# Attention scores of a hybrid decoder trunk: the keys' low halves on all 128 rows, and the low-by-low product added

## The chip, the core and the metric

The kernel runs on one core of a Trainium2 chip. The metric is device time in microseconds (us) of one execution; the time of a kernel is the median of its runs. One execution is also recorded by the hardware profiler; its rows are what this text reads.

## The reference

A decoder trunk of two layers over 512 tokens of width 1024, all in float32. Layer 0 mixes with a gated MLP and an RWKV-7 time mix and ends with a dense SwiGLU. Layer 1 mixes with a sparse attention (eight query heads, two key/value heads of 64 channels, that is, four query heads to a key/value head) and a gated short convolution, and ends with a mixture of eight experts of which each token uses two. What the change touches are the scores of two of the attention's three branches, the selected blocks and the window; with 512 tokens both reach every earlier token, so they differ only in their keys and values:

```python
ss = jnp.einsum('bhgqd,bhqnld->bhgqnl', qr, kg).astype(f32)
ps = _masked_softmax(ss.reshape(...) * scale, ms)
...
sw = jnp.einsum('bhgqd,bhkd->bhgqk', qr, kwb).astype(f32) * scale
pw = _masked_softmax(sw, mw)
```

qr are the queries and kg, kwb the keys, both after a partial rotation by position; a score is a sum over 64 channels.

## The kernel before, in words

TensorE multiplies in a reduced float32 format ("fp32r" in the rows). To keep float32 accuracy, an operand is split: the high half is the value copied into fp32r (on ScalarE), the low half is the difference (a subtraction on VectorE, `split`, line 107). A product is then three matmuls into one PSUM bank, high by high, high by low, low by high (`mm3`, line 125; lines 127 to 129 in the rows).

Layer 1's mix (`layer1_mix`, line 682) runs in this order in the program: constants, projections of keys and queries (`nsa_proj`), two projections that feed the compressed branch (`compress`), then `attend` for four query blocks of 128 tokens (tb = 0 to 3), four blocks of the short convolution (`conv`, three projections each) and the output rows. The program order is not the order in the queues: instructions are traced by a tile framework whose planner orders each engine's queue at build time, by a priority and by when an instruction is ready in its plan, and sets the semaphores. Conv projections therefore stand between score matmuls in TensorE's queue, as fillers (rows with `pmm`, lines 127 to 129).

For a score the 64 channels of a key/value head g lie on one half of the 128 rows. `nsa_proj` and `stacked` (lines 748 and 737) lay out the operands:

- Queries, tile `qq` per head b and key/value head g: the high half of the query lies on the rows of g, its low half on the other 64 rows (copied there by a DMA on the POOL queue, lines 769 and 770).
- Keys' high halves, tile `kk` per branch and g: on the rows of g, and a copy on the other 64 rows (DMAs on POOL, lines 759 and 760).
- Keys' low halves, tile `klo` per branch: one tile of 128 rows in which each g has its own 64 rows.

`attend` (line 805) works through two branches, four heads b and two key/value heads g. A score block is 128 queries by n keys, n = 128, 256, 384, 512 for tb = 0 to 3, and takes two matmuls into one of two PSUM banks `sc`: line 821 on all 128 rows (query high and low, each with the key's high half) and line 822 on the 64 rows of g (query high with key low). There are 64 such pairs, 16 in each query block. VectorE then adds the mask and takes the row minimum (line 824), ScalarE the exponential (826), VectorE scales (834), TensorE transposes (839), ScalarE copies out of PSUM (842), and TensorE multiplies by the values (847).

Weights come through SP's DMA queue into three `wraw` buffers (line 955), in 512 KB units; a unit is split into `whi` and `wlo` (lines 108 and 109) and feeds 24 matmuls. Line 975 in `moe_consts` loads a gain row `grow`, 1024 values spread over 128 rows; `moe_consts` runs before `layer1_mix`, and the row is read only in `router` (lines 1023 and 1026), at the end of layer 1's mix. A tile that shares a tag with another takes its place in memory, so its first write waits for the last reader of the other.

Of the kernel before, what the change touches and what calls it, by code (L numbers as in the profile page):

```python
# [9 lines left out]
F32 = mybir.dt.float32  # L10
F32R = mybir.dt.float32r
# [7 lines left out]
T = 512  # L19
D = 1024  # L20
# [47 lines left out]
class Body:  # L68
# [613 lines left out]
    def layer1_mix(self):  # L682
        nc, tc, I = self.nc, self.tc, self.I
        with ExitStack() as ctx:
            pool = lambda name, bufs, **kw: ctx.enter_context(tc.tile_pool(name=name, bufs=bufs, **kw))
            self.cp1, self.wk1, self.pa = pool("n_const", 1), pool("n_work", 2), pool("n_psum", 1, space=PSUM)
            self.nsa_consts()
            self.nsa_proj()
            self.compress()
            self.acc = [self.cp1.tile([128, 2, T], F32, tag="zc%d" % i, name="acc") for i in range(2)]  # L690
            for tb in range(NTB):
                self.attend(tb)
            yd = [self.conv(b) for b in range(3)]
            self.out_rows(I["w_out1a"][0:2], yd[0:2])
            yd.append(self.conv(3))
            yc = []
            for q in range(4):
                hi = self.cp1.tile([128, T], F32R, tag="q%d" % q, name="ych")
                lo = self.cp1.tile([128, T], F32R, tag="qq%da" % q, name="ycl")
                self.split(hi, lo, self.acc[q // 2][:, q % 2, :])  # L700
                yc.append((hi, lo))
            self.out_last(I["w_out1"], yc, I["w_out1a"][2:4], yd[2:4])
# [34 lines left out]
    def stacked(self, src, lo, name):  # L737
        nc, cp = self.nc, self.cp1
        out = []
        for g in range(2):  # L740
            p = slice(g * 64, g * 64 + 64)
            t = cp.tile([128, T], F32R, name=name + "ab"[g])
            nc.scalar.activation(t[p], src[p], AF.Copy)
            nc.vector.tensor_sub(lo[p], src[p], t[p].bitcast(F32))
            out.append(t)
        return out

    def nsa_proj(self):
        nc, I, cp, wk = self.nc, self.I, self.cp1, self.wk1
        V, S, G = nc.vector, nc.scalar, nc.gpsimd  # L750
        unit = lambda i: self.unit(I["w_in1"][i])
        near, far = slice(0, 64), slice(64, 128)
        self.kk, self.klo = [], []
        pss = self.proj_first([self.ahead[0], self.unit(I["w_in1"][1], G, raw=self.ahead[1])], lambda: self.bank("sc", 2))
        for i in range(2):
            src = self.roped(pss[i], wk.tile([128, T], F32, tag="wA", name="qtmp"))
            lo = cp.tile([128, T], F32R, name="klo%d" % i)
            kk = self.stacked(src, lo, "kk%d" % i)
            nc.gpsimd.dma_start(kk[0][far], kk[0][near])
            nc.gpsimd.dma_start(kk[1][near], kk[1][far])  # L760
            self.kk.append(kk)
            self.klo.append(lo)
        self.qs, self.qq = [], []
        for b in range(4):
            q = cp.tile([128, T], F32, name="q%d" % b)
            src = self.roped(self.proj_block(unit(2 + b)), q)
            lo = wk.tile([128, T], F32R, tag="pt", name="qlo", bufs=PTB)
            qq = self.stacked(src, lo, "qq%d" % b)
            nc.gpsimd.dma_start(qq[0][far], lo[near])
            nc.gpsimd.dma_start(qq[1][near], lo[far])  # L770
            self.qs.append(q)
            self.qq.append(qq)
        self.vsw = cp.tile([128, NTB, 256], F32, name="vsw")
        self.gat = cp.tile([128, NTB, 8, 3], F32, name="gat")
        units = [unit(6 + i) for i in range(3)]
        for tb in range(NTB):
            t = slice(tb * 128, (tb + 1) * 128)
            ps = self.psum()
            for kb in range(KB):
                wh, wl = units[kb // 3]  # L780
                n = slice((kb % 3) * 280, (kb % 3) * 280 + 280)
                self.mm3(ps[:, 0:280], self.xh[:, kb, t], self.xl[:, kb, t], wh[:, n], wl[:, n],
                         kb == 0, kb == KB - 1)
            V.tensor_copy(self.vsw[:, tb, :], ps[:, 0:256])
            S.activation(self.gat[:, tb].rearrange("p h b -> p (h b)"), ps[:, 256:280], AF.Sigmoid)
        self.zc = []
        for j in range(2):
            ps = self.proj_block(unit(9 + j))
            raw = wk.tile([128, T], F32, tag="wA", name="craw")
            S.activation(raw, ps, AF.Copy)  # L790
            z = cp.tile([128, 16, 2, 32], F32, name="zc%d" % j)
            G.memset(z[:, :, :, 31:32], 0.0)
            for g in range(2):
                zp = wk.tile([128, T], F32, tag="wB", name="zp")
                src = raw[g * 64:g * 64 + 64, :]
                nc.sync.dma_start(zp[0:64, :], src)
                nc.sync.dma_start(zp[64:128, 0:T - 1], src[:, 1:T])
                zv = zp.rearrange("p (n l two) -> p l n two", l=8, two=2)[:, :, :, 0]
                for lh in range(2):
                    V.tensor_tensor(z[:, lh * 8:lh * 8 + 8, g, 0:31], zv[:, :, lh:lh + 31],  # L800
                                    self.cpos[:, j, lh * 8:lh * 8 + 8].unsqueeze(2).broadcast_to([128, 8, 31]),
                                    op=ALU.add)
            self.zc.append(z)

    def attend(self, tb):
# [6 lines left out]
        for br in range(2):  # L812
            sm = self.sm.tile([128, 8], F32, name="smm", bufs=2)
            mn = self.sm.tile([128, 8], F32, name="mn", bufs=2)
            pt = [[wk.tile([128, 2, 4, 128], F32, name="pt", bufs=PTB) for _ in range((tb + 2) // 2)] for _ in range(2)]
            for b in range(4):
                es = []
                for g in range(2):
                    i = b * 2 + g
                    ps = self.bank("sc", 2)  # L820
                    mm(ps[:, 0:n], self.qq[b][g][:, t], self.kk[br][g][:, 0:n], start=True, stop=False)
                    mm(ps[:, 0:n], self.qq[b][g][half[g], t], self.klo[br][half[g], 0:n], start=False, stop=True)  # L822
                    e = wk.tile([128, T], F32, name="prob", bufs=4)
                    V.tensor_tensor_reduce(e[:, 0:n], ps[:, 0:n], self.dmask[:, 512 - n:512], scale=-0.125,  # L824
                                           scalar=3e38, op0=ALU.add, op1=ALU.min, accum_out=mn[:, i:i + 1])
                    S.activation(e[:, 0:n], e[:, 0:n], AF.Exp, bias=mn[:, i:i + 1], scale=-1.0,
                                 accum_out=sm[:, i:i + 1])
                    es.append(e)
                rc = sm[:, b * 2:b * 2 + 2]
                V.tensor_scalar(rc, rc, 1e-30, None, op0=ALU.max)  # L830
                V.reciprocal(rc, rc)
                for g in range(2):
                    e = es[g]
                    V.tensor_scalar(e[:, 0:n], e[:, 0:n], rc[:, g:g + 1], self.gat[:, tb, g * 4 + b, br + 1:br + 2],
                                    op0=ALU.mult, op1=ALU.mult)
                    ps = self.bank("tr", 2)
                    for kb in range(tb + 1):
                        k = slice(kb * 128, (kb + 1) * 128)
                        nc.tensor.transpose(ps[:, k], e[:, k], self.ident)
                    for j, d in enumerate(pt[g]):  # L840
                        m = min(2, tb + 1 - 2 * j)
                        S.activation(d[:, 0:m, b, :], ps[:, j * 256:j * 256 + m * 128].rearrange("p (k t) -> p k t", k=m),
                                     AF.Copy)
            for kb in range(tb + 1):
                for g in range(2):
                    c = br * 128 + g * 64
                    mm(po[half[g], :], self.vsw[:, kb, c:c + 64],
                       pt[g][kb // 2][:, kb % 2].rearrange("p b t -> p (b t)"), start=(br == 0 and kb == 0), stop=False)
# [109 lines left out]
    def moe_consts(self, cp):  # L958
# [12 lines left out]
        def load(name, shape, src):  # L971
            t = cp.tile(shape, F32, name=name)
            nc.sync.dma_start(t, src)
            return t
        self.grow = load("grow", [128, D], I["o_norm_ffn"].broadcast_to([128, D]))
        wr = load("wr", [128, KB, 8], I["w_router"])
        gcol = load("gcol", [128, KB], I["ffn_gain"])
        self.wr = cp.tile([128, KB, 32], F32, name="wrg")
# [623 lines left out]
```

## Time and profile before

| | |
|---|---|
| median of 3 runs | 1592.73 us (1589.03 to 1598.78) |
| the profiled execution | 1590.39 us |
| its span, first to last instruction | 1588.6 us, mean granted TensorE clock 0.983 |
| TensorE matmuls | 1516.7 us busy (95%), 9891 instructions |
| VectorE | 931.8 us busy (59%) |
| ScalarE | 765.4 us busy (48%) |
| GpSimd (POOL) | 180.0 us busy (11%) |
| DMA | 243.48 MB, 153 GB/s on average |

Times in the rows are microseconds from the span's start, unless marked ns. PE is TensorE's matmul, PEld its weight load, DVE VectorE, ACT ScalarE, POOL GpSimd, SP SyncE; a q behind a name is the engine's instruction queue, on which DMAs are issued. L822 is line 822. "out<-in" names the tiles, with digits at the end left out in some places (`klo` is klo0 or klo1). The end of a matmul is modelled by the profiler, its start is not: matmuls overlap in the rows, and the distance between two starts tells what one costs. The granted clock (PEclk) is a share of 2.4 GHz. A row of the table by stage has the window, its length, the busy us (and instructions) of PE, PEld, DVE, ACT and POOL, the granted clock, the DMA share and GB/s.

### The profile page before, as it was taken

Reading aid. Unit: us, or ns where it says so; the run is one execution under the profiler, and the core shown is the slowest. Engines: PE = TensorE matmul, PEld = TensorE weight load, DVE = VectorE, ACT = ScalarE, POOL = GpSimd, SP = SyncE. Lnnn points to the kernel's source line nnn. Section 1 sums busy time; section 2 is a strip of 40 time slices with the busy share of each in tenths; the row PEclk is TensorE's granted clock in tenths of the full one; section 3 lists DMA queues with packets and bytes.
Section 4 is the critical chain, followed back from the end, with each engine's and each line's share of the span. In section 5 each row is a group of like instructions: output and inputs, shape, how many; then the busy total and the mean of one; then the engine's idle time right before and its main releaser. Section 6 shows DMA issues by size and latency. Waiting matters only on the chain. (4 is left out here: it accounts for less than half of the span.)

```text
span 1588.6 us, 25120 instructions
## 1 busy us (share of the span) xinstructions
PE 1516.7 (95%) x9891; PEld 1144.9 (72%) x9891; DVE 931.8 (59%) x1491; ACT 765.4 (48%) x1184; POOL 180.0 (11%) x164
## 2 busy tenths in 40 slices
PE   6999999999999999999999999969999999999985
PEld 5777767778888888888776657846767776786763
DVE  5566456646333333224645666557777887787795
ACT  5444343344222322123435563326667777676663
POOL 1122021100000000000300000031000000000087
PEclk9999999999999999999998999979999999999998
DMA  5111111212222222221642002246778898797792
GB/s 205 67 42 45 58 67 59 71 48 85 101 99 100 93 93 93 97 97 35 181 139 96 27 14 75 72 171 252 282 285 310 310 399 297 275 376 299 271 363 81
DMA packets 74964, 243.48 MB, mean 153 GB/s; under 512 B 10000, under 2 KB 13584, under 8 KB 74832
## 3 DMA queue, kind: packets, MB, share of 16 engines
q1 hardware_dynamic: 69632, 225.72, 38.8%
q0 software_dynamic: 5200, 15.99, 3.0%
q8 instruction: 84, 1.38, 0.3%
q14 instruction: 48, 0.39, 0.1%
HBM read 229.88 MB, written 9.18 MB: 150 GB/s over the span
## 5 line engine op out<-in xcount | busy, mean ns | idle before, releaser
L108 ACT ACTIVATE whi<-wraw 128x1024 fp32r<-128x1024 f32 (+1 forms) x406 | 414.7, 1026 | 450.8 <-PE pmm L128 128.2
L109 DVE TENSOR_TENSOR wlo<-wraw,whi 128x1024 fp32r<-128x1024 f32 (+1 forms) x401 | 479.0, 1207 | 256.9 <-ACT whi L108 251.4
L128 PE MATMUL pmm<-xl,whi 128*128 128x512 f32 x640 | 258.2, 403 | 0.0
L129 PE MATMUL pmm<-xh,wlo 128*128 128x512 f32 x640 | 257.7, 403 | 0.1
L127 PE MATMUL pmm<-xh,whi 128*128 128x512 f32 x640 | 256.9, 401 | 0.0
L1205 PE MATMUL pe<-whi,xg 128*128 128x512 f32 (+1 forms) x768 | 238.7, 383 | 1.6 <-PEq L1242 0.2
L1205 PEld LDWEIGHTS pe<-whi,xg 128*128 128x128 f32 x768 | 143.3, 188 | 38.0 <-issue 11.2
L1205 PE MATMUL pe<-wlo,xg 128*128 128x512 f32 (+1 forms) x384 | 147.1, 383 | 6.3 <-DVE wlo L109 6.0
L127 PEld LDWEIGHTS pmm<-xh,whi 128*128 128x128 f32 x640 | 120.4, 188 | 31.8 <-issue 6.9
L128 PEld LDWEIGHTS pmm<-xl,whi 128*128 128x128 f32 x640 | 120.6, 188 | 28.6 <-issue 3.6
L129 PEld LDWEIGHTS pmm<-xh,wlo 128*128 128x128 f32 x640 | 120.5, 188 | 26.7 <-issue 2.8
L1205 PE MATMUL pe<-whi,act 128*128 128x512 f32 x352 | 117.4, 404 | 0.6
L1205 PEld LDWEIGHTS pe<-wlo,xg 128*128 128x128 f32 x384 | 72.5, 189 | 23.2 <-DVE wlo L109 12.8
L1205 PEld LDWEIGHTS pe<-whi,act 128*128 128x128 f32 x352 | 66.4, 189 | 20.2 <-issue 4.0
L1205 PE MATMUL pe<-wlo,act 128*128 128x512 f32 x176 | 70.3, 399 | 2.7 <-DVE wlo L109 2.7
L127 PE MATMUL pd<-whi,fah 128*128 128x512 f32 x176 | 69.7, 396 | 0.0
L128 PE MATMUL pd<-wlo,fah 128*128 128x512 f32 x176 | 69.6, 395 | 0.0
L129 PE MATMUL pd<-whi,fal 128*128 128x512 f32 x176 | 69.6, 395 | 0.0
L109 POOL TENSOR_TENSOR wlo<-wraw,whi 128x1024 fp32r<-128x1024 f32 x5 | 13.4, 2686 | 433.8 <-ACT whi L108 433.8
L645 DVE TENSOR_TENSOR sg<-sg,pmm 128x512 f32<-128x512 f32 x21 | 14.4, 688 | 71.7 <-PE pmm L129 71.7
L1149 POOL DMA_INDIRECT xm<-xd,slot x16 | 18.1, 1134 | 277.8 <-PE pe L1167 266.8
L824 DVE CUSTOM_DVE_ANT_0 prob<-pa_sc,dmask 128x128 f32<-128x128 f32 (+3 forms) x64 | 31.1, 489 | 31.5 <-PE pa_sc L822 22.6
(594 smaller groups left out, 2296.4 us busy)
## 6 DMA issues: line engine op xcount, KB each, us to landing
wraw<-moe_gu SPq DMA_DIRECT2D x128, 512.0 KB, 9.2
wraw<-moe_dn SPq DMA_DIRECT2D x88, 512.0 KB, 7.0
wraw<-ffn_gu SPq DMA_DIRECT2D x50, 512.0 KB, 3.2
wraw<-moe_gv SPq DMA_DIRECT2D x64, 384.0 KB, 8.0
wraw<-w_in SPq DMA_DIRECT2D x45, 512.0 KB, 3.3
wraw<-ffn_dn SPq DMA_DIRECT2D x22, 512.0 KB, 3.2
wraw<-w_out SPq DMA_DIRECT2D x12, 512.0 KB, 3.2
wraw<-cmp_w SPq DMA_DIRECT2D x8, 512.0 KB, 3.8
```

The source lines that it names most:

```text
L108: self.nc.scalar.activation(hi, src, AF.Copy)
L109: (sub or self.nc.vector).tensor_sub(lo, src, hi.bitcast(F32))
L127: mm(ps, lh, rh, start=start, stop=False)
L128: mm(ps, lh, rl, start=False, stop=False)
L129: mm(ps, ll, rh, start=False, stop=stop)
L645: nc.vector.tensor_mul(sg, sg, pu)
L824: V.tensor_tensor_reduce(e[:, 0:n], ps[:, 0:n], self.dmask[:, 512 - n:512], scale=-0.125, scalar=3e38, op0=ALU.add, op1=ALU.min, accum_out ...
L1149: nc.gpsimd.indirect_dma_start(out=x[0:n, i, :], out_offset=None, in_=self.xd, in_offset=bass.IndirectOffsetOnAxis(ap=(self.slot[0:n, e - ...
L1205: mm(py[nh][:, 0:wide], x[:, k, ia, :], w[iw][:, nh * wide:(nh + 1) * wide], start=(k + j == 0), stop=(k == n - 1 and j == 2))
```

## The change

The keys' low halves get the same layout as the high halves: per branch and key/value head a tile with the 64 channels on the rows of g and a copy on the other 64 rows. The tile of g = 0 is the old `klo0` or `klo1`; those of g = 1 are two halves of a new tile `klox` of 128 x 2 x 512. Four more DMAs on POOL make the copies. Line 822's matmul then runs on all 128 rows, and as the query's low half lies on the other rows, it adds the product of low by low. In `stacked` the caller gives a tile per g; for the queries it is the same tile twice. The gain row `grow` leaves `moe_consts`; it takes the memory of `klox` after the attention and is loaded in `layer1_mix` behind the last `attend`.

```diff
--- before.py
+++ after.py
@@ -690,6 +690,8 @@
             self.acc = [self.cp1.tile([128, 2, T], F32, tag="zc%d" % i, name="acc") for i in range(2)]
             for tb in range(NTB):
                 self.attend(tb)
+            self.grow = self.cp1.tile([128, D], F32, tag="klox", name="grow")
+            nc.sync.dma_start(self.grow, I["o_norm_ffn"].broadcast_to([128, D]))
             yd = [self.conv(b) for b in range(3)]
             self.out_rows(I["w_out1a"][0:2], yd[0:2])
             yd.append(self.conv(3))
@@ -741,7 +743,7 @@
             p = slice(g * 64, g * 64 + 64)
             t = cp.tile([128, T], F32R, name=name + "ab"[g])
             nc.scalar.activation(t[p], src[p], AF.Copy)
-            nc.vector.tensor_sub(lo[p], src[p], t[p].bitcast(F32))
+            nc.vector.tensor_sub(lo[g][p], src[p], t[p].bitcast(F32))
             out.append(t)
         return out
 
@@ -752,12 +754,14 @@
         near, far = slice(0, 64), slice(64, 128)
         self.kk, self.klo = [], []
         pss = self.proj_first([self.ahead[0], self.unit(I["w_in1"][1], G, raw=self.ahead[1])], lambda: self.bank("sc", 2))
+        other = cp.tile([128, 2, T], F32R, tag="klox", name="klox")
         for i in range(2):
             src = self.roped(pss[i], wk.tile([128, T], F32, tag="wA", name="qtmp"))
-            lo = cp.tile([128, T], F32R, name="klo%d" % i)
+            lo = [cp.tile([128, T], F32R, name="klo%d" % i), other[:, i, :]]
             kk = self.stacked(src, lo, "kk%d" % i)
-            nc.gpsimd.dma_start(kk[0][far], kk[0][near])
-            nc.gpsimd.dma_start(kk[1][near], kk[1][far])
+            for a, b in (kk, lo):
+                nc.gpsimd.dma_start(a[far], a[near])
+                nc.gpsimd.dma_start(b[near], b[far])
             self.kk.append(kk)
             self.klo.append(lo)
         self.qs, self.qq = [], []
@@ -765,7 +769,7 @@
             q = cp.tile([128, T], F32, name="q%d" % b)
             src = self.roped(self.proj_block(unit(2 + b)), q)
             lo = wk.tile([128, T], F32R, tag="pt", name="qlo", bufs=PTB)
-            qq = self.stacked(src, lo, "qq%d" % b)
+            qq = self.stacked(src, [lo, lo], "qq%d" % b)
             nc.gpsimd.dma_start(qq[0][far], lo[near])
             nc.gpsimd.dma_start(qq[1][near], lo[far])
             self.qs.append(q)
@@ -819,7 +823,7 @@
                     i = b * 2 + g
                     ps = self.bank("sc", 2)
                     mm(ps[:, 0:n], self.qq[b][g][:, t], self.kk[br][g][:, 0:n], start=True, stop=False)
-                    mm(ps[:, 0:n], self.qq[b][g][half[g], t], self.klo[br][half[g], 0:n], start=False, stop=True)
+                    mm(ps[:, 0:n], self.qq[b][g][:, t], self.klo[br][g][:, 0:n], start=False, stop=True)
                     e = wk.tile([128, T], F32, name="prob", bufs=4)
                     V.tensor_tensor_reduce(e[:, 0:n], ps[:, 0:n], self.dmask[:, 512 - n:512], scale=-0.125,
                                            scalar=3e38, op0=ALU.add, op1=ALU.min, accum_out=mn[:, i:i + 1])
@@ -972,7 +976,6 @@
             t = cp.tile(shape, F32, name=name)
             nc.sync.dma_start(t, src)
             return t
-        self.grow = load("grow", [128, D], I["o_norm_ffn"].broadcast_to([128, D]))
         wr = load("wr", [128, KB, 8], I["w_router"])
         gcol = load("gcol", [128, KB], I["ffn_gain"])
         self.wr = cp.tile([128, KB, 32], F32, name="wrg")
```

## Rows read from the trace of the kernel before

**Rows 1.** Table by stage; columns as told above.

```profile
817.00:851.00 34.00, 32.03 (x139) 20.33 (x137) 15.96 (x66) 17.30 (x47) 1.19 (x6) 0.85 0.48 155
851.00:918.00 67.00, 67.00 (x328) 43.62 (x328) 46.70 (x175) 39.64 (x127) 0.10 (x1) 1.00 0.12 40
918.00:952.00 34.00, 33.96 (x155) 18.89 (x153) 22.47 (x71) 21.73 (x65) 0.00 (x0) 1.00 0.05 17
952.00:1022.00 70.00, 69.98 (x335) 55.48 (x333) 42.78 (x69) 26.12 (x46) 0.38 (x1) 1.00 0.21 76
...
910.00:930.00 20.00, 20.00 (x88) 11.44 (x89) 14.81 (x50) 12.31 (x38) 0.00 (x0) 1.00 0.08 27
```

**Rows 2.** Timeline of PE, block 1: start, length, line, tiles, stationary, moving size.

```profile
860.16 0.28 PE L821 MATMUL pa_sc<-kk0a,qq2a 128*128 128x256 f32 x1
860.36 0.38 PE L822 MATMUL pa_sc<-klo,qq2a 64*128 64x256 f32 x1
860.68 0.50 PE L129 MATMUL pmm<-xh,wlo 128*128 128x512 f32 x1
861.02 0.28 PE L821 MATMUL pa_sc<-kk0b,qq2b 128*128 128x256 f32 x1
```

**Rows 3.** Timeline of PE, block 3, two pairs with no filler between.

```profile
927.18 0.50 PE L821 MATMUL pa_sc<-kk0b,qq1b 128*128 128x512 f32 x1
...
928.03 0.49 PE L821 MATMUL pa_sc<-kk0a,qq2a 128*128 128x512 f32 x1
```

**Rows 4.** Timeline, block 0, two pairs with no filler between.

```profile
823.70 0.33 PE L821 MATMUL pa_sc<-kk0a,qq1a 128*128 128x128 f32 x1
...
824.21 0.33 PE L821 MATMUL pa_sc<-kk0b,qq1b 128*128 128x128 f32 x1
```

**Rows 5.** Timeline of PE, full-array matmuls alone, 256 and 512 columns.

```profile
761.70 0.28 PE L127 MATMUL pa_sc<-xh,whi 128*128 128x256 f32 x1
...
762.40 0.28 PE L127 MATMUL pa_sc<-xh,whi 128*128 128x256 f32 x1
...
956.17 0.39 PE L127 MATMUL pmm<-xh,whi 128*128 128x512 f32 x1
...
958.00 0.39 PE L129 MATMUL pmm<-xh,wlo 128*128 128x512 f32 x1
```

**Rows 6.** Lines 821, 822: count, ns min/median/max, first, last start; who waited.

```profile
L821 PEld LDWEIGHTS pa_sc<-kk0a,qq0a x4: 188/192/195, 817.2 to 918.2; 128*128 128x128 f32 x4
...
L822 PEld LDWEIGHTS pa_sc<-klo,qq0a x8: 182/183/183, 817.6 to 935.3; 64*128 64x128 f32 x8
...
  DVE prob L824: 22.6, 28
```

**Rows 7.** Line 744, the last of the four low halves of the keys.

```profile
L744 DVE TENSOR_TENSOR klo<-roped,kk1b x1: 689/689/689, 772.9 to 772.9; 64x512 fp32r<-64x512 f32 x1
```

**Rows 8.** Timeline of POOL, [idle before <-releaser].

```profile
772.05 0.51 POOL L760 DMA_DIRECT2D kk1b<-kk1b  x1
774.79 2.38 POOL L733 TENSOR_TENSOR qcos<-q,rope 128x512 f32<-128x512 f32 x1 [2.22 <-ACT q L727]
```

**Rows 9.** Timeline of SP's queue; lengths span all issues of a row.

```profile
270.98 0.33 SPq L158 DMA_DIRECT2D grow<-e_norm_ffn  x1
...
279.41 0.38 SPq L592 DMA_DIRECT2D lnr<-sgu_rows  x1
...
851.27 3.11 SPq L955 DMA_DIRECT2D wraw<-w_in  x2
...
919.36 41.34 SPq L955 DMA_DIRECT2D wraw<-w_out1a  x2
```

**Rows 10.** Timeline of PE, the last score matmul.

```profile
950.73 0.50 PE L822 MATMUL pa_sc<-klo,qq3b 64*128 64x512 f32 x1
```

**Rows 11.** Tile grow, its first reader in the router.

```profile
L1023 DVE SCALAR_TENSOR_TENSOR xs<-h,ss,grow x3: 1284/1286/1289, 1022.7 to 1042.1; 128x1024 f32<-128x1024 f32 x3
```

**Rows 12.** Tile kza, its last reader on PE.

```profile
L543 PE MATMUL prw<-gna,kza x64: 218/218/268, 119.7 to 270.6; 64*64 64x64 f32 x64
```

## The prediction, made before the change was run

> **What bounds the kernel now.** I read the page first: TensorE is the busiest engine, but its busy share says little, since ends of matmuls are modelled. So I went to the table by stage, cut where the attention begins and ends. There the reader is to see that from 851 to 952 us TensorE has next to no idle time, while VectorE is busy 46.70 + 22.47 = 69.2 of 101 us and the DMA share is 0.12 and 0.05 [rows 1]: the attention of query blocks 1 to 3 goes at the pace of TensorE's queue. From 817 to 851 us (block 0) TensorE idles 1.97 us and the mean granted clock is 0.85, so a part of that stretch ran at the lower level, 1.2 GHz; there other engines have a say. From 952 to 1022 us TensorE is full again, and a time saved before it moves everything behind it forward.
>
> Busy time does not tell what one matmul costs in a full queue; the distance from one start to the next does. So the third view is TensorE's queue in order of time. In [rows 2] a score pair (L821 on 128 rows, L822 on 64) stands among filler matmuls of the conv projections. From the start of L821 at 860.16 to the next L821 at 861.02 it does one pair of 256 columns and one filler of 512 columns, in 0.86 us. Full-array matmuls alone, one after the other, take far less: from 761.70 to 762.40 us six of 256 columns start, 0.117 each; from 956.17 to 958.00 eight of 512 columns, 0.229 each [rows 5]. These accumulate in one bank too, so it is not the accumulation that costs. At full-array pace the same three would take 2 x 0.117 + 0.229 = 0.463. The change of row count, there and back, costs 0.86 - 0.463 = 0.40 us per pair. At 512 columns without filler a pair takes 928.03 - 927.18 = 0.85 [rows 3] against 2 x 0.229 = 0.458: 0.39. So it does not hang on the size or the neighbour. The size of it, 0.195 per change, is near the duration of one weight load, 0.183 [rows 6]: a load that otherwise lies under the matmul before it lies bare.
>
> **The change part by part.** *The second score matmul on 128 rows.* 64 pairs, 16 per query block. For blocks 1 to 3 both costs above frame the third size (384 columns): 48 x 0.39 = 18.7 us of TensorE time go. For block 0 (128 columns) a pair takes 824.21 - 823.70 = 0.51 [rows 4]. A stream of full-array f32r matmuls of 128 columns I did not find; by the row at 256 columns one costs at most 0.117 and at least half of that, 0.06. I take 0.117, since a weight load of the same size stands in front of each: 0.51 - 0.234 = 0.28 per pair, 16 x 0.28 = 4.4 us. Gross: 23.1 us.
>
> The doubled rows themselves I cost at nothing, since the 64-row matmul streams as many columns as the 128-row one. Bounds: nothing, and, if the longer loads lay bare, 64 times the difference between a load of 128 rows, 0.192, and one of 64, 0.183 [rows 6]: 0.6 us.
>
> The Trainium skill ("TensorE: Matmul & The Clock Gate", section "LDWEIGHTS (loading the stationary operand)") puts a load at its columns over 1.2, 107 ns for 128 columns, whatever the rows. An estimate by that page: 128 bare loads x 0.107 = 13.7 us gross in place of 23.1. The rows differ from it, 0.183 us for a load [rows 6] and 0.195 per change from start to start, and the measurement decides; no number below uses the page's.
>
> *What of it is kept.* TensorE's gain counts as far as the next engine follows. The next one is VectorE: L824 waited for L822 28 times, 22.6 us in all [rows 6], so VectorE is now often the early one, and its 32 us of idle time in 851 to 952 us hold 18.7. Afterwards it would be busy 69.2 of 82.3 us, 84%. That is more than it shows in any stretch of the attention (14.81 of 20 us, 74%, in the fullest one [rows 1]), and with two score banks some of the gain turns into TensorE waiting for a bank. Upper bound: all 18.7. Lower bound: VectorE can't pass 74%; then the stretch takes 69.2 / 0.74 = 93.5 instead of 101, a gain of 7.5. I take 85%, 15.9 us, nearer to the upper end because the order in the queues stays much as it is and TensorE doesn't idle there at all now. Of block 0's 4.4 us I keep 2.9: the first branch's eight pairs (2.2) come before the compression's matmuls in one queue; the second branch lies where TensorE idles and the clock is low, and I keep 0.7 of its 2.2 (bounds 0 and 2.2).
>
> *Four more copies of low halves on POOL.* They take the place behind kk1b's issue and the low half made last, at 772.9 + 0.69 = 773.6 us [rows 7]. The rotation product of the next query block begins on POOL at 774.79, after 2.22 idle [rows 8]. An issue like kk1b's is 0.51 us [rows 8], so four are 2.0 us and nearly fit the idle time; what doesn't fit delays that product by at most 2.0, and behind it VectorE's addition of the two rotation products and the weight splits queued there, which feed TensorE's next projection. The scores that read the copies start at 817.2 [rows 6], over 40 us later, and until then TensorE has projections to do. The VectorE subtractions are the same twelve; only the tile they write changes. Cost: 0, bounds 0 and 2.0; I enter 0.5.
>
> *The gain row for the router moves.* It is now the first load on SP after layer 0; afterwards it takes the slot of the second low tile, so it waits for the last score matmul, at 950.73 now [rows 10], about 930 then. Its first reader is at 1022.7 [rows 11]: 70 us of room. What stands behind it in SP's queue must be asked: the load issued at 919.36 and its successor, some 41 us later [rows 9]. If it stands between those two, nothing is late. A row of the same kind shows how the planner treats such a load: the gain row into the slot of kza is issued at 270.98, right after that slot's last reader at 270.6 [rows 12], while the loads for the later gates follow at 279.41 [rows 9], although the gates stand before it in the program. SP's order follows readiness in the plan and not the program. Cost 0. At the front the other constants go out one issue earlier; no reader of theirs is on TensorE's path there, so 0 as well. Bounds: 0 and the slower rival below.
>
> Sum: 15.9 + 2.9 - 0.5 = 18.3 us. From the profiled execution's own 1590.39: 1572.1. The median of the three runs shown is 2.3 us above that execution, so on the scale of the median: 1592.73 - 18.3 = 1574.4, and I say 1574.
>
> **The rivals.** *VectorE takes over.* The changes of row count go, but the softmax chain becomes the bound: 7.5 us in blocks 1 to 3 and 1 in block 0, 1584. For it: 84% is asked of VectorE. Against it: its waits for TensorE in that stretch are longer than what it must give up. 0.22.
>
> *The rows don't matter.* The bare load hangs on something else in the pair, and only the second matmul's row count changes: 0, 1593. By the rows it would be the place of L822 in the pair that costs. Against it: L821 after a filler and a filler after L822 both lose time, on either side of the 64-row matmul. 0.07. The Trainium skill ("TensorE: Matmul & The Clock Gate", section "Why this matters for your kernels") says that one matmul with a short contraction takes the same time as one with 128 rows; by that rule filling the array brings nothing here. The trace agrees for the streaming, but not for what it costs to go over and back.
>
> *Slower: the gain row blocks SP.* If the planner puts it on SP before the loads that the conv fillers need, these wait behind it until the last score matmul. Six loads are issued from 851.27 to 919.36 [rows 9]; each feeds 24 matmuls of 0.229, 5.5 us, so 33 us of filler would run after the attention instead of inside it, and the attention alone would take VectorE's 93.5: 126.5 instead of 101, 25 more, 1618. It decides from the second load on (7.5 gained against 5.5 per load). For it: the load is asked for right behind the attention, ahead of the conv. Against it: the row at 270.98. 0.05.
>
> **How the numbers follow.** Forecast 0.64, the three rivals 0.22, 0.07 and 0.05, another order of the queues with up to 10 us either way 0.02. The forecast alone ranges from 1570 (all of 23.1 kept) to 1579 (two thirds of 18.7 and the first branch of block 0, less 0.5 for POOL). For the whole I add the spread of the runs below (the fastest is 3.7 under the median) and reach over the VectorE case: 1565 to 1590, which leaves out the last two rivals and a tail. A measurement of this kernel can tell about 1% (16 us) from no change. Over 1% faster is 0.62 of the 0.64; within 1% are the rest of it, the VectorE case and the one without effect, 0.32; slower 0.06.
>
> **What would show it.** Right: L822 with 128 rows; a pair at 512 columns in about 0.46 us and the filler behind it at 0.229; the stretch from block 1's first score to block 3's last some 16 us shorter; TensorE still without idle time there; the gain row on SP near the last score, no weight load late. The VectorE case: L821 waiting for L824. Wrong altogether: pairs still at 0.85.

## The result, and the profile after

The kernel after takes 1571.5 us (median of 4 runs, 1569.49 to 1579.64) against 1595.41 for the kernel before (4 runs). The medians are 23.9 us apart, a quotient of 0.9850; the ratio computed from all these runs is 0.9868, with a 95% interval of 0.9845 to 0.989 in which that quotient lies. Measured again beside other kernels it was 0.9882 (0.9857 to 0.9908). 1.2 to 1.5% faster, then, some 19 to 24 us; 1574 with 1565 to 1590 was predicted. The profiled execution takes 1569.49 us, 20.9 less than that of before.

From the first score on, TensorE's queue has the same instructions in the same order in both kernels, so the traces can be laid side by side. The scores start at 817.5 us before and 816.6 after; the four query blocks and the whole stretch, in us, from first score to first score (the last block to its last score):

| kernel | block 0 | block 1 | block 2 | block 3 | all scores |
|---|---|---|---|---|---|
| before | 35.86 | 27.97 | 37.11 | 32.32 | 133.26 |
| after | 33.09 | 22.56 | 31.26 | 26.85 | 113.76 |
| gain | 2.77 | 5.41 | 5.85 | 5.47 | 19.50 |

Blocks 1 to 3 are the firm part of it. They take 97.40 us in before, layout_row64 and grow_only, the three kernels with 64 rows everywhere and this order, and 80.61 to 80.68 in after, after_again, full_zero and sgu_full, the four with 128 rows everywhere. Block 0 is not firm: it takes 35.86, 35.64 and 34.39 in those three, and 33.09, 34.12, 33.62 and 33.02 in those four.

So 19.5 of the 20.9 us come from the scores' stretch; 0.9 lies in front of it and 0.5 behind it. A difference of 0.9 in front says nothing: among the profiles of this study the first score stands anywhere from 810.0 to 819.9 us.

The timeline of TensorE's queue after, blocks 1 and 3, with the columns of [rows 2]:

```profile
864.43 0.28 PE L825 MATMUL pa_sc<-kk1b,qq1b 128*128 128x256 f32 x1
864.55 0.28 PE L826 MATMUL pa_sc<-klox,qq1b 128*128 128x256 f32 x1
864.67 0.40 PE L129 MATMUL pmm<-xh,wlo 128*128 128x512 f32 x1
864.90 0.40 PE L127 MATMUL pmm<-xh,whi 128*128 128x512 f32 x1
...
907.92 3.22 PE L851 MATMUL pa_po<-pt,vsw 128*64 128x512 f32 x12
911.07 0.50 PE L825 MATMUL pa_sc<-kk0b,qq1b 128*128 128x512 f32 x1
911.41 0.40 PE L826 MATMUL pa_sc<-klox,qq1b 128*128 128x512 f32 x1
911.64 0.40 PE L825 MATMUL pa_sc<-kk0a,qq2a 128*128 128x512 f32 x1
911.88 0.39 PE L826 MATMUL pa_sc<-klo,qq2a 128*128 128x512 f32 x1
912.11 0.38 PE L924 MATMUL pa_tr<-ident,cs 128*128 128x128 f32 x2
```

Line 826 is the old 822, now 128 rows. One pair of 256 columns and one filler take 864.90 - 864.43 = 0.47 us, where [rows 2] have 0.86; a pair of 512 columns takes 912.11 - 911.64 = 0.47, where [rows 3] have 0.85. Nothing is left of the 0.39 in these two pairs: every start follows the one before it by about what a matmul takes in a stream of full-array ones, 0.117 or 0.229 [rows 5]. (The pair before the second one shows something else: its L826 starts 0.34 after its L825, which stands behind the 64-column matmuls of line 851. More on this under what to carry to other kernels.)

The table by stage, after, answers to [rows 1] (the second window is the scores of blocks 1 to 3):

```profile
817.00:851.00 34.00, 30.91 (x155) 21.00 (x155) 17.95 (x78) 19.98 (x57) 1.10 (x5) 0.90 0.53 170
849.70:930.30 80.60, 80.55 (x460) 57.77 (x460) 64.90 (x232) 56.42 (x181) 0.10 (x1) 1.00 0.11 38
```

VectorE is now busy 64.90 of 80.60 us, 81%, against 74% in the fullest 20 us of before, and TensorE still has no idle time by this view. That TensorE is closer to waiting is seen in the waits around blocks 1 to 3 (before from 850 to 970 us, after from 851 to 932; us in total, times, longest), in one such wait in the queue of the weight loads after, and in who waited for line 826:

```profile
PEld pa_sc L821 <- DVE mn L824: 0.3, 1, 0.3
```

```profile
PEld pa_sc L825 <- DVE mn L828: 2.7, 10, 0.3
```

```profile
928.48 0.19 PEld L825 LDWEIGHTS pa_sc<-kk1b,qq2b 128*128 128x128 f32 x1 [0.29 <-DVE mn L828]
```

```profile
L826 PEld LDWEIGHTS pa_sc<-klo,qq0a x8: 187/189/192, 816.6 to 917.0; 128*128 128x128 f32 x8
...
  DVE prob L828: 13.9, 14
```

The weight load of the first score matmul waited 10 times for VectorE to free a score bank, 2.7 us, where it had waited once, 0.3 us. Such a load then begins together with its matmul, and the next start comes later: in the pair of the third line L826's matmul starts at 928.82, 0.34 after L825's, where a stream has 0.229. The last line is the other direction: over all blocks VectorE waited for scores 14 times, 13.9 us, in place of 28 times and 22.6 us [rows 6].

POOL's queue after, where [rows 8] were, and SP's queue after, where [rows 9] were:

```profile
771.20 0.52 POOL L763 DMA_DIRECT2D klo<-klo  x1
...
773.28 0.52 POOL L764 DMA_DIRECT2D klox<-klox  x1
773.98 1.78 POOL L735 TENSOR_TENSOR qcos<-q,rope 128x512 f32<-128x512 f32 x1 [0.17 <-ACT q L729]
```

```profile
904.44 0.33 SPq L959 DMA_DIRECT2D wraw<-w_out1a  x1
930.76 0.33 SPq L694 DMA_DIRECT2D grow<-o_norm_ffn  x1
939.69 0.33 SPq L959 DMA_DIRECT2D wraw<-w_out1a  x1
```

The four copies fill the hole on POOL; the rotation product behind them still waits for ScalarE, not for POOL's own queue. The gain row is issued 0.42 us after the last score matmul (930.34), between the two loads of output weights.

### The profile page after: what moved, and what is told of

Same layout as the page of the kernel before. It is cut to its first block, busy times and chain, and to the rows that moved or that the text cites. A ratio compares the mean times of both kernels' runs of the same rounds, so it can differ in the third digit from the quotient of the medians.

```text
span 1567.6 us, 25129 instructions
## 1 busy us (share of the span) xinstructions
PE 1496.7 (95%) x9891; PEld 1142.4 (73%) x9891; DVE 930.8 (59%) x1491; ACT 764.4 (49%) x1184; POOL 182.4 (12%) x168
## 5 line engine op out<-in xcount | busy, mean ns | idle before, releaser
L1215 PE MATMUL pmm<-wraw,xr 128*32 128x512 f32 (+1 forms) x384 | 41.3, 560 | 0.0
```

Source lines behind the costliest of these rows:

```text
L1215: mm(pr[q:q + 32, 0:wide], xr[:, k, :], raws[i, k][:, nh * wide:(nh + 1) * wide], start=(k < 2), stop=(k + 2 >= n))
```

## The experiments

All ratios are to the kernel before, run beside them on the same chip. All but grouped_row64 have, from the first score on, the order of before and after in TensorE's queue; the fourth column is the stretch from the first score to the first expert matmul, within which all fillers lie.

| kernel | ratio, 95% interval | all scores | to the experts |
|---|---|---|---|
| before | | 133.26 | 255.2 |
| after | 0.9868 (0.9845 to 0.989) | 113.76 | 235.5 |
| layout_row64 | 1.0019 (1.0003 to 1.0035) | 133.04 | 255.1 |
| half_full | 0.9946 (0.9925 to 0.9966) | 123.49 | 246.3 |
| full_zero | 0.9888 (0.9866 to 0.991) | 114.29 | 236.1 |
| grow_only | 0.9992 (0.9971 to 1.0013) | 131.80 | 255.0 |
| grouped_row64 | 0.994 (0.9918 to 0.9962) | 127.25 | 243.5 |
| after_again | 0.9882 (0.9857 to 0.9908) | 114.79 | 236.0 |
| sgu_full | 0.9826 (0.9797 to 0.9856) | 113.64 | 235.1 |

### layout_row64: everything but the rows

```diff
-mm(ps[:, 0:n], self.qq[b][g][:, t], self.klo[br][g][:, 0:n], start=False, stop=True)
+mm(ps[:, 0:n], self.qq[b][g][half[g], t], self.klo[br][g][half[g], 0:n], start=False, stop=True)
```

> The kernel after, but the second score matmul runs on the 64 rows of its key/value head again; the copies of the low halves, the new tile and the moved gain row stay, and all queues keep the order of the kernel after. My theory (the change of row count lays a weight load bare, twice per pair): the whole gain goes, ratio to before 0.998 to 1.002; a pair of 512 columns takes 0.85 us from start to start again and the scores from the first to the last take 133 us as before, against 114 after. Rival (the gain comes from the new layout, the moved gain row or the slightly other order of the queues): it stays, ratio 0.987.

The whole gain goes: 1.0019, and the scores take 133.04 us. A pair in block 3, timeline of TensorE's queue of this kernel:

```profile
927.64 0.49 PE L825 MATMUL pa_sc<-kk0b,qq1b 128*128 128x512 f32 x1
928.06 0.49 PE L826 MATMUL pa_sc<-klox,qq1b 64*128 64x512 f32 x1
928.48 0.49 PE L825 MATMUL pa_sc<-kk0a,qq2a 128*128 128x512 f32 x1
```

0.84 per pair, 0.42 to the second matmul and 0.42 from it. The copies, the tile and the moved gain row bring nothing; the number of rows in one matmul does it all. The interval lies just above 1, by 0.03%; what that would be I did not follow.

### half_full: 128 rows in one branch only

```diff
+r = slice(0, 128) if br == 0 else half[g]
+mm(ps[:, 0:n], self.qq[b][g][r, t], self.klo[br][g][r, 0:n], start=False, stop=True)
-mm(ps[:, 0:n], self.qq[b][g][:, t], self.klo[br][g][:, 0:n], start=False, stop=True)
```

> The kernel after with 128 rows in the second score matmul only in the first of the two branches; the second branch runs on 64 rows as before. Same order in all queues. My theory: each pair pays for itself, so half of the gain stays, ratio 0.992 to 0.995; the pairs of 512 columns of the first branch at 0.46 us, those of the second at 0.85. Rival (the gain comes once, by keeping up with the engine behind, so that the second half of the pairs adds little): ratio near 0.988 or near 0.999.

Half of it stays: 0.9946, and the scores take 123.49 us, 9.8 of the 19.5 us less. Both kinds of pair stand in one trace, block 3, first the first branch, then the second:

```profile
916.88 0.39 PE L825 MATMUL pa_sc<-kk0a,qq1a 128*128 128x512 f32 x1
917.11 0.39 PE L827 MATMUL pa_sc<-klo,qq1a 128*128 128x512 f32 x1
917.34 0.39 PE L128 MATMUL pmm<-xl,whi 128*128 128x512 f32 x1
...
939.50 0.51 PE L825 MATMUL pa_sc<-kk1a,qq2a 128*128 128x512 f32 x1
939.94 0.49 PE L827 MATMUL pa_sc<-klo,qq2a 64*128 64x512 f32 x1
940.36 0.50 PE L128 MATMUL pmm<-xl,whi 128*128 128x512 f32 x1
```

0.46 and 0.86. Blocks 1 to 3 take 88.57 us, 8.8 of the 16.7 less. Each pair pays for itself; the second half of the gain was not eaten by VectorE.

### full_zero: no copies, no low-by-low product

```diff
-for a, b in (kk, lo):
-    nc.gpsimd.dma_start(a[far], a[near])
-    nc.gpsimd.dma_start(b[near], b[far])
+nc.gpsimd.dma_start(kk[0][far], kk[0][near])
+nc.gpsimd.dma_start(kk[1][near], kk[1][far])
+V.tensor_sub(lo[0][far], src[far], src[far])
+V.tensor_sub(lo[1][near], src[near], src[near])
```

> All 128 rows in the second score matmul, but the other 64 rows of the keys' low tiles are zeros made on VectorE: it leaves out the low-by-low product and the four copies on POOL. My theory: what rows hold makes no difference and the copies were hidden, so it is as fast as the kernel after, ratio to before 0.985 to 0.990, scores in 114 us. Rival (the copies on POOL cost something, up to the 2.0 us of their issues): up to 2 us faster than after, and the first score that much earlier. Against both: four more VectorE instructions of 0.7 us, near 773 us, where VectorE is not full.

0.9888, scores in 114.29 us: as after, within what can be told. Rows of zeros serve as well as rows of data, and the four copies cost nothing that shows. The low-by-low product comes with the layout; time is neither paid for it nor saved by it.

### grow_only: the gain row moved, nothing else

```diff
+both = cp.tile([128, 2, T], F32R, tag="klox", name="klox")
 ...
-lo = cp.tile([128, T], F32R, name="klo%d" % i)
+lo = both[:, i, :]
 ...
+self.grow = self.cp1.tile([128, D], F32, tag="klox", name="grow")
+nc.sync.dma_start(self.grow, I["o_norm_ffn"].broadcast_to([128, D]))
```

(the last two lines behind the last `attend`; the old load is gone)

> The kernel before with nothing but the gain row moved: both low tiles of the keys become halves of one tile, the gain row takes its place after the last score. 64-row matmuls as before. My theory: the load is hidden at either place, ratio 0.998 to 1.002, and it is issued between the two loads of output weights. Rival (512 KB less in front of layer 1, 0.5 us of loads on SP): 0.5 to 1 us faster, which cannot be told from no change by the median, but by an earlier first score (817.5 before, 816.6 after).

0.9992 (0.9971 to 1.0013), and 255.0 us from the first score to the experts: no change. (The scores take 131.80 us, 1.46 less than before, all of it in block 0.) The first score stands at 815.9; as after_again, with the same front as after, has it at 813.8, the place of the first score in one profile decides nothing on the half microsecond that the rival asked for. It stays open, below what can be measured.

### grouped_row64: fewer changes of row count, with 64 rows

```diff
-for g in range(2):
-    i = b * 2 + g
-    ps = self.bank("sc", 2)
-    mm(ps[:, 0:n], self.qq[b][g][:, t], self.kk[br][g][:, 0:n], start=True, stop=False)
-    mm(ps[:, 0:n], self.qq[b][g][half[g], t], self.klo[br][half[g], 0:n], start=False, stop=True)
+pss = [self.bank("sc", 2) for _ in range(2)]
+for g in range(2):
+    ahead = mm(pss[g][:, 0:n], self.qq[b][g][:, t], self.kk[br][g][:, 0:n], start=True, stop=False)
+with self.tc.issue_after(ahead.ins):
+    for g in range(2):
+        mm(pss[g][:, 0:n], self.qq[b][g][half[g], t], self.klo[br][half[g], 0:n], start=False, stop=True)
```

> The kernel before with 64 rows in the second matmul, but both first matmuls of a head come ahead of its two second ones, so that the two 64-row matmuls can follow each other. In TensorE's queue the 64 second matmuls stand in 39 runs in place of 64, so there are 78 changes of row count in place of 128. My theory (the change of row count costs 0.195 us): 50 x 0.195 = 9.8 us less TensorE time, of which some 85% shows, ratio 0.994 to 0.996; a 64-row matmul right behind a 64-row one starts without the bare load. It may be somewhat more, if the two use different halves of the array at once, or less, since the other engines' order differs a little. Rival (each 64-row matmul costs 0.39 us more, wherever it stands): no gain, ratio 0.999 to 1.002.

This is the run that tells a dear kind of matmul from a dear change between kinds. All 64 matmuls on 64 rows are there, as before; only their neighbours differ. 0.994, and 11.7 us less from the first score to the experts. (The blocks can't be compared one by one here, since the planner laid the fillers elsewhere.) Two pairs of block 1, TensorE's queue of this kernel:

```profile
852.97 0.38 PE L820 MATMUL pa_sc<-kk0a,qq1a 128*128 128x256 f32 x1
853.19 0.28 PE L820 MATMUL pa_sc<-kk0b,qq1b 128*128 128x256 f32 x1
853.40 0.38 PE L823 MATMUL pa_sc<-klo,qq1a 64*128 64x256 f32 x1
853.41 0.38 PE L823 MATMUL pa_sc<-klo,qq1b 64*128 64x256 f32 x1
853.72 0.50 PE L128 MATMUL pmm<-xl,whi 128*128 128x512 f32 x1
```

Two pairs in 0.75 us. The first L823 starts 0.21 after the full matmul before it, in place of 0.117, and the matmul behind the two 0.31 after them, as behind a single one in [rows 2]; the second L823 starts 0.01 after the first. The two lie on different halves of the rows and run side by side. So a 64-row matmul is not dear in itself; a change to or from it is. How the 11.7 us divide this run doesn't tell: by the count that was put down, 50 changes fewer are worth 9.8 us of TensorE time at most, and in the 25 places where two 64-row matmuls follow each other the second one's streaming time is saved as well.

### sgu_full: the same cure in layer 0

```diff
-mm(o, ltri[0:1, :], ln[0:1, 2, :], start=False, stop=True)
+mm(o, self.ident, ln[:, 2, :], start=False, stop=True)
```

This is the kernel after and this edit in `sgu` (line 624); after_again, the kernel after unchanged, stood beside it.

> The kernel after, once more, beside the two below on the same chip: ratio to before 0.985 to 0.990.

> The kernel after, and the same cure at another place: in the gated MLP of layer 0 the bias is added by a matmul on one row behind a full one, 16 times (L624). It becomes a full-array matmul with the identity, whose moving operand is the bias that already lies on all rows; the sum is the same. My theory: at each of the some 15 places the change of row count there and back costs what it costs in the scores; the four starts of a product and its bias lie at 0.21 us each now and a full-array one of this kind at 0.11, so 16 x 0.4 = 6 us of TensorE time go, of which what TensorE bounds there shows: 3 to 6 us faster than after, ratio to before 0.983 to 0.986. Rival (there the recurrence bounds, not TensorE): as after.

0.9826 (0.9797 to 0.9856) against 0.9882 for after_again: by the medians 1567.63 against 1573.9 us, 6.3 less, a little more than the 3 to 6 that were expected; the two intervals just miss each other. In the traces the mechanism is plain; a bias matmul (L624) and a product (L623), each two rows of the trace, TensorE's queue of the kernel after, then of this kernel:

```profile
276.98 0.48 PE L624 MATMUL pmm<-lnr,ltri 1*128 1x128 f32 x2
277.40 0.49 PE L623 MATMUL pmm<-sw,sg 128*128 128x128 f32 x2
277.81 0.48 PE L624 MATMUL pmm<-lnr,ltri 1*128 1x128 f32 x2
```

```profile
275.68 0.38 PE L624 MATMUL pmm<-lnr,ident 128*128 128x128 f32 x2
275.90 0.39 PE L623 MATMUL pmm<-sw,sg 128*128 128x128 f32 x2
276.13 0.39 PE L624 MATMUL pmm<-lnr,ident 128*128 128x128 f32 x2
```

Bias and product take 0.83 us with one row and 0.45 with 128: 0.38 per change there and back, at another place, with another row count and full float32 operands. 16 of these are 6.1 us, and the medians of six runs each show about that. The two profiled executions do not: 1566.92 us here and 1567.01 for after_again. Here the first score comes at 810.0 us, 3.8 earlier and ahead of the other eight profiles, but what stands behind the last score takes 641.5 us against 636.7.

## Why the prediction was right

*The term that carried it.* 0.39 us per pair, read as the distance between starts with and without 64-row neighbours [rows 2 to 5], is what the change gives back: 0.47 for what took 0.86, 0.47 for what took 0.85. layout_row64 and half_full show that it hangs on the row count of that matmul and on each pair alone; grouped_row64 shows that it belongs to the change and not to the matmul. The rival in which the rows don't matter is out.

*What the 0.195 is made of.* The prediction took it for one bare weight load, since 0.195 is near the 0.183 that a load lasts in the rows. The loads do lie bare, but the rows divide the 0.195 otherwise. The queue of the weight loads before, around the pair of [rows 2], and one load in the stream of [rows 5]:

```profile
860.36 0.18 PEld L822 LDWEIGHTS pa_sc<-klo,qq2a 64*128 64x128 f32 x1 [0.24 <-issue]
860.67 0.19 PEld L129 LDWEIGHTS pmm<-xh,wlo 128*128 128x128 f32 x1
860.78 0.19 PEld L821 LDWEIGHTS pa_sc<-kk0b,qq2b 128*128 128x128 f32 x1
```

```profile
761.70 0.19 PEld L128 LDWEIGHTS pa_sc<-xl,whi 128*128 128x128 f32 x1
```

In the stream a load begins with the matmul before its own (761.70, its matmul 0.117 later). At a change it begins with its own matmul (860.36 and 860.67), and the next load can begin 0.11 later (860.78), well before the row of 0.19 ends. The pair of [rows 2] divides the same way: L822 starts 0.20 after L821, some 0.09 more than in a stream; the filler 0.32 after L822, 0.20 more; the next L821 0.34 after the filler, 0.11 more. So a change costs some 0.09 before the load begins and 0.11 for the load. The estimate of 0.107 per bare load that the prediction set aside fits the second part; what it leaves out is the first, and what fills that 0.09 no run here shows. The forecast doesn't hang on this, since its price was read from starts.

*What was kept.* Blocks 1 to 3 gained 5.41 + 5.85 + 5.47 = 16.7 us, 89% of the 18.7; I had taken 85%. That share was a judgement between two bounds and came from no row, so that it fits is partly luck. Of the 2.0 us that are missing, 0.3 are the way back of the last pair, which lies behind the end of the stretch, and some 1 us, by an estimate of 0.1 for each of the 10 waits shown above, is L825 waiting for a bank, as the prediction had said; the rest is not traced. VectorE did pass the 74% on which the lower bound rested, it reached 81% of the stretch; the rival in which it takes over is out, though the waits show it closer to being the bound.

*Block 0.* 2.77 against 2.9 is partly a match by chance: profiles with the same score matmuls differ there by up to 1.5 us, and the means of the three 64-row and the four 128-row kernels above are 1.8 us apart. TensorE idles 3.1 of 34 us there now and 1.97 before.

*POOL and the gain row.* The half microsecond entered for the copies did not show: full_zero without them is no faster, and the rotation product behind them waits for ScalarE. The gain row stands on SP where it was put, so the slower rival is out; grow_only shows no cost or gain for it.

*The size.* 18.3 were forecast, 19.5 came in the scores' stretch and 20.9 between the two profiled executions: 16.7 against 15.9 in blocks 1 to 3, 2.77 against 2.9 in block 0, 0.5 not seen on POOL, and 1.4 outside the stretch, less than profiles of the same code differ by there. The medians are further apart, 23.9: with a fourth run that of the kernel before is 1595.41 in place of 1592.73. What could not be told from the rows is whether VectorE would follow at 81%; the whole distance between the bounds 7.5 and 18.7 hung on it.

## What to carry to other kernels

Look in TensorE's queue for matmuls on fewer rows than their neighbours: a short contraction or a one-row bias among full ones cost 0.38 to 0.40 us there and back here, and nothing in the busy times says so; the distance from start to start does. Fill the rows (with the missing product, with zeros, or by an identity in place of a row of ones), or put the short ones next to each other, on different halves of the rows. What that freed here counted where TensorE's queue was full (blocks 1 to 3, 0.05 us idle in 80.60), and as far as VectorE, which empties PSUM, could follow; in block 0, where TensorE idles, less of it showed.

A change of the column count may cost the same; no run here tests it. Line 851's matmuls are 64 columns wide on all 128 rows, in every kernel of this study. Behind them the next score pair pays about 0.11: 911.41 - 911.07 = 0.34 in place of 0.229.

## What had not been expected

Two 64-row matmuls on different halves of the rows started 0.01 us apart (853.40 and 853.41) and shared their streaming time, though they write two different banks and belong to different key/value heads; so grouping alone, without any fill, won half of what the change won. And the part ahead of the scores, all but the same in these kernels, put the first one anywhere from 813.8 to 819.9 us in the profiles without the sgu edit: one span alone can't settle a change of a few microseconds, while a stretch cut around the change repeated to within about 1.5 us (113.76, 114.79, 114.29 and 113.64 us; 133.26, 133.04 and 131.80), and blocks 1 to 3 alone, where TensorE's queue is full, to within 0.1.
